# One pair of heads moved between the recurrent tiles, and the last x^T block loaded behind two products, in a hybrid decoder block

## Chip, cores and metric

The kernel runs on one core of a Trainium2 chip. The metric is the time of one execution on the device in microseconds. The engines have the profile's names: PE (TensorE matmul), PEld (its weight loads), DVE (VectorE), ACT (ScalarE), POOL (GpSimd), SP (SyncE, which issues most DMAs).

## What is computed

One decoder block on x of 2048 tokens by 1024, in float32. Cut to what matters here:

```
h = rms_norm(x)
z = h @ w_in                       # 1024 x 2560
q, k, v (512 each), xr (512), gr (512) = split(z)
attn = dilated_attention(q, k, v)  # 8 heads of 64, three dilations
xr   = causal_depthwise_conv(xr)   # 4 taps
rec  = rg_lru(xr) * gelu(gr)       # gated linear recurrence over tokens
m = concat(attn, rec) @ w_out
x = x + rms_norm(m)
x = x + rms_norm(squared_relu_mlp(rms_norm(x)))
```

The recurrence is h = a·h + u along the tokens, with a and u made from two gates (block-diagonal matmuls, then tanh). The MLP is 1024 to 4096 to 1024.

## The kernel before

**Products.** Each float32 operand is split into a high and a low part, both of the matmul's fp32r type, and a product is three matmuls: high by high, low by high, high by low (`product`, L206 to L208). Channels of z are cut into 20 tiles of 128, tokens into two halves `hf` of 1024, each of two blocks b of 512. A product z*hf*_*ct*_*b* takes channel tile ct and one block: 8 slices of the 1024 inputs by 3 matmuls, 24 matmuls of 128x512 into one PSUM bank. The tag "P" of these banks has two buffers, so a product can start only when the one two before it has been read. Tiles 0 to 3 are q, 4 to 7 k, 8 to 11 v (one for each pair of heads), 12 to 15 the recurrence's input, 16 to 19 its gate.

**Weights.** `load_w` brings a tile's weights in two raw halves ("wraw", two buffers), casts them on ACT (wH, L56) and subtracts (wL, L57). The engine of the subtraction is `self.lo`, POOL at first. Behind BETWEEN (below) it is set to VectorE. The low parts of q and k (zl) go by the same setting. After each step of products `load_ahead` loads the next step's first weights.

**Input.** `load_x(tb)` loads eight raw tiles of x^T for 512 tokens (xr, L157), six into the low part's own later slots and two into "wraw", and makes hH (ACT, L180) and hL (VectorE, L181). `spread_norm(tb)` turns the tokens' norm factors into a row for all partitions (four dg, L194, four matmuls, one copy). Blocks 2 and 3 are the second half.

**Steps.** `qkv(hf, pr)`, letter q, makes six products for a pair of heads, multiplies each by the norm row on VectorE (zn, L233 and L236), and stores q, k and v to DRAM. `recurrent(hf, (c,))`, letter r, makes for each block a product of tile 12 + c (VectorE reads it into xr, L312), a convolution (POOL L315, three VectorE steps L318), the two gate matmuls (pr, L321, and pi, L323), ACT functions, the scan (L339), a product of tile 16 + c (VectorE reads it into gr, L343), gelu (POOL L346 to L348, ACT L349, VectorE L350 and L351) and a store. `attend(pr)`, letter a, is the first half's attention for a pair: scores S and SB, masking on VectorE (L422), exp on ACT (L428), transposes pT (L401), output sums oA and oB (L589, L648), normalisers pst (L680).

**What sets the order.** Three strings give the program order:

```
ORDER = "q00 r02 q01 a0 r03 q02 a1 q03 x2 x3 a2 q10 a3"
BETWEEN = "r10 r11 r12 r13"
LATER = "q11 q12 q13"
```

The two digits behind a letter are the half and the pair or tile; x is a load of x^T with its norm row. The scheduler written into the kernel (`Plan` and `Machine`) then orders the instructions of all five engines by its own table of costs and by when each result is needed. A step moved in a string moves several hundred instructions on each engine. q10 has its own order of products: q and k of block 2 before those of block 3.

After BETWEEN the recurrence's pool is closed, and in its room `load_wo(0)` loads W_out: eight loads of 512 KB (woL, L800), each cast in two halves to woH and subtracted. Then the steps of LATER run, five steps of `early_factors` (sums of W_ff tiles, e*j*_*m*) behind each, and what is left of these at the end. The first products that use W_out follow (m, L865 to L867). m0_0_1 means: half 0, token tile 0, columns 1.

Of the kernel before, what the change touches and what calls it, by code (L numbers as in the profile page):

```python
# [39 lines left out]
def f32(ap):  # L40
    return ap.bitcast(F32)
# [12 lines left out]
def split(nc, hi, lo, src, lo_eng=None):  # L54

    return (nc.scalar.copy(out=hi, in_=src),  # L56
            (lo_eng or nc.vector).tensor_tensor(out=lo, in0=src, in1=f32(hi), op=ALU.subtract))  # L57
# [31 lines left out]
class Project:  # L89
# [118 lines left out]
            pe.matmul(z, lo[:, k, :], hh, start=False, stop=(k == KT - 1))  # L208
        return z

    def qkv(self, hf, pr):

        nc, p, scr = self.nc, self.p, self.scr
        v, pe = nc.vector, nc.tensor
        last = hf == 0 and pr == NP - 1
        steps = [(k, b) for k in range(3) for b in range(NBH)]
        if last:

            steps = [(0, 0), (0, 1), (1, 0), (2, 0), (1, 1), (2, 1)]
        elif hf and pr == FIRST:  # L220

            steps = [(0, 0), (1, 0), (0, 1), (1, 1), (2, 0), (2, 1)]
        ws = {}
        for kind, b in steps:
                ct = 4 * kind + pr
                if kind not in ws:
                    ws[kind] = self.load_w(hf, ct)
                w = ws[kind]
                cs = slice(b * TB, (b + 1) * TB)
                z = self.product(hf, ct, w, b)  # L230
                zn = self.pa.tile([P, TB], F32, tag="t512", bufs=3, name=f"zn{hf}_{ct}_{b}")
                if kind == 0:
                    v.scalar_tensor_tensor(out=zn, in0=z, scalar=-(HD ** -0.5), in1=self.bc[b], op0=ALU.mult,  # L233
                                           op1=ALU.mult)
                else:
                    v.tensor_tensor(out=zn, in0=z, in1=self.bc[b], op=ALU.mult)  # L236
                if kind < 2:
                    zh = self.pa.tile([P, TB], F32R, tag="zh", bufs=1, name=f"zh{hf}_{ct}_{b}")
                    zl = self.pa.tile([P, TB], F32R, tag="zl", bufs=1, name=f"zl{hf}_{ct}_{b}")
                    self.cst["pool"] = split(nc, zh, zl, zn, lo_eng=self.lo)[1]  # L240
                    dst = scr["q" if kind == 0 else "k"][hf][pr]
                    for u in range(2):
                        nc.sync.dma_start(out=f32(dst[u, 0, :, cs]), in_=f32(zh[u * HD:(u + 1) * HD, :]))
                        nc.sync.dma_start(out=f32(dst[u, 1, :, cs]), in_=f32(zl[u * HD:(u + 1) * HD, :]))
                else:
                    pt = self.bank("X", f"vt{hf}_{ct}_{b}")
# [597 lines left out]
class OutProj:  # L844
# [1092 lines left out]
def trunk(tc, x, xT, g1, g2, g3, g4, w_in, conv_w, conv_b, w_r, b_r, w_i, b_i, lam, w_out, w1, w2,  # L1937
# [4 lines left out]
    def sb(name, side):  # L1942
        return tc.tile_pool(name=name, bufs=1, side=side, reuse_waits="tile")
# [5 lines left out]
    with (  # L1949
# [46 lines left out]
        def load_wo(hf, between=lambda: None):  # L1996
            return load_w_out(tc, wst.enter_context(sb(f"wo{hf}", "right")), scr["wout"], hf, order, cst, between)

        with contextlib.ExitStack() as st:
            p1a = st.enter_context(sb("p1a", "left"))  # L2000
            p1 = st.enter_context(sb("p1", "left"))
            lst = contextlib.ExitStack()
            pl = lst.enter_context(sb("lru", "left"))
            pj = Project(tc, p1, p1a, pl, bank, cst, scr, x, xT, g1, w_in)
            pj.recurrent_consts(conv_w, conv_b, w_r, b_r, w_i, b_i, lam)
            with sb("x0", "right") as px:
                w = {12: pj.load_start(12, px)}
                z = pj.product(0, 12, w[12], 0, "B")
                w[16] = pj.load_w(0, 16, nc.vector, px)
                w[13] = pj.load_w(0, 13, nc.vector, px)  # L2010
                pj.load_norm(0, px)
                pj.spread_norm(0)
                pj.recurrent_block(0, 0, 0, w[12], w[16], px, z)
                w[17] = pj.load_w(0, 17, nc.gpsimd, px)
                pj.load_x(1, px)
                pj.recurrent_block(0, 1, 0, w[13], w[17], px)
                pj.load_norm(1, px)
                pj.spread_norm(1)
                for i in range(2):
                    pj.recurrent_block(0, i, 1, w[12 + i], w[16 + i], px)  # L2020
                pj.load_norm(2, px)
                pj.load_norm(3, px)
            products = [(t[0], *map(int, t[1:])) for t in f"{ORDER} {BETWEEN} {LATER}".split() if t[0] in "qr"]

            copies = [(scr["wout"][k], w_out[k]) for k in order]
            for j in range(NJ):
                copies += [(scr["w2"][j][:, 0], w2[2 * j][:, 0:TB]),
                           (scr["w2"][j][:, 1:3], w2[2 * j + 1].rearrange("p (a d) -> p a d", a=2))]

            def run(steps):  # L2030
                for kind, *arg in [(t[0], *map(int, t[1:])) for t in steps.split()]:
                    if kind == "q":
                        pj.qkv(*arg)
                    elif kind == "r":
                        pj.recurrent(arg[0], (arg[1],))
                    elif kind == "a":
                        attend(*arg)
                    else:
                        pj.load_x(*arg)
                        pj.spread_norm(*arg)  # L2040
                    n = 8 if kind == "r" and arg[0] else 1 if len(copies) > 2 * NJ else 0
                    with tc.issue_after(cst["pool"].ins):
                        for dst, src in copies[:n]:
                            nc.gpsimd.dma_start(out=dst, in_=src)
                    del copies[:n]
                    if kind in "qr":
                        products.pop(0)
                        if products:
                            nxt, hf, i = products[0]
                            pj.load_ahead(hf, i if nxt == "q" else 12 + i)  # L2050

            place = {"S": ("B", "B"), "pT": ("T", "T"), "o": ("O", "T")}
            with sb("at0", "right") as pa:
                attend = attention(tc, pa, lambda k, n: bank(place[k][0], n), cst, scr, 0, mask_a, mask_b, pa)
                run(ORDER)
            pg = per.enter_context(sb("g2", "right"))
            sh = Shared(pg, bank)
            run(BETWEEN)
            lst.close()
            wo = load_wo(0)  # L2060
            pj.lo = nc.vector
            early = [early_factors(nc, sh, scr, w1, j) for j in range(2)]
            for step in LATER.split():
                run(step)
                for _ in range(5):
                    if early and next(early[0], True):
                        early.pop(0)
            for rest in early:
                for _ in rest:
                    pass  # L2070
            ready = [mix_columns(nc, sh, scr, 0, order, t) for t in range(2)]
# [85 lines left out]

FIRST = 0
SH = 2
ORDER = "q00 r02 q01 a0 r03 q02 a1 q03 x2 x3 a2 q10 a3"  # L2160
BETWEEN = "r10 r11 r12 r13"
LATER = "q11 q12 q13"


def _by_residue(t):
# [53 lines left out]
```

## Time and profile before

| | |
|---|---|
| median of 3 runs | 2226.05 us (2224.66 to 2227.85) |
| profiled execution | 2225.13 us, span 2223.4 us, mean granted clock 0.99 |
| PE busy | 97% of the span, 10264 matmuls |
| DVE, ACT, POOL busy | 69%, 56%, 20% |
| DMA | 473.51 MB, 213 GB/s mean |
| tail of attention 2; end of the last product of z | 341 to 359 us; 637 us |

The profiled execution is 0.9 us shorter than the median. The steps lie in its span as follows: a1 to about 290 us, x2, x3 and a2 to 359, q10 to 388, a3 to 424, r10 to r13 from 412 to 529, q11 to q13 from 529 to 637, the m products after that. Read the table of windows by PE's busy time against a window's length (the rest is idle) and by PEclk (a share below 1 makes the same matmuls take longer).

### The profile page before, as it was taken

The numbers are of one execution on the slowest core, as the hardware profiler recorded it, in microseconds if no ns is written. First come the engines' busy times: TensorE is split into PE (matmuls) and PEld (weight loads), VectorE is DVE, ScalarE is ACT, GpSimd is POOL, SyncE is SP. The second block draws the span as 40 slices with busy tenths as digits, with TensorE's granted clock in tenths as the row PEclk, the third lists the DMA queues.
The fourth block names the chain that finished last, engine by engine and source line by source line (L and its number), as shares of the span: only waits on it lengthen the run. The fifth ranks groups of instructions, "written<-read, shape, count | busy, mean of one in ns | idle before, by whom it ended". The sixth has DMA issues, their size and how long they took to land.

```text
span 2223.4 us, 30885 instructions
## 1 busy us (share of the span) xinstructions
PE 2155.1 (97%) x10264; PEld 1770.1 (80%) x10264; DVE 1529.9 (69%) x2910; ACT 1235.2 (56%) x2487; POOL 454.5 (20%) x536
## 2 busy tenths in 40 slices
PE   8999998988999999999999999999999999999998
PEld 6787877766888788888788888877878888888887
DVE  6858765897647867676567777777766565755556
ACT  6646655645434555555566767754455555654442
POOL 4652434386212100000001111113200000000003
PEclk9999998999999999999999999999999999999999
DMA  7574675247954677779777787786553434876665
GB/s 252 159 220 149 199 236 182 70 163 265 333 167 150 241 269 270 288 269 333 261 220 242 206 246 213 218 256 198 191 175 139 161 132 163 305 219 191 194 194 180
DMA packets 224116, 473.51 MB, mean 213 GB/s; under 512 B 23428, under 2 KB 78756, under 8 KB 217684
## 3 DMA queue, kind: packets, MB, share of 16 engines
q1 hardware_dynamic: 195140, 337.52, 47.7%
q0 software_dynamic: 28816, 134.01, 16.9%
q8 instruction: 81, 1.33, 0.2%
q14 instruction: 79, 0.65, 0.1%
HBM read 337.09 MB, written 151.13 MB: 220 GB/s over the span
## 4 chain that ended last, share of the span: by engine, by line
PE 81%; DVE 9%; ACT 4%; DMA 3%; issue 2%; POOL 1%; SPq 0%; DVEq 0%; ACTq 0%; POOLq 0%
PE o L1230 8%; PE o L1232 8%; PE o L1231 8%; PE za L1081 5%; PE za L1082 5%; PE za L1080 5%; PE z L206 4%; PE z L207 4%; PE z L208 4%; PE m L867 3%; PE m L866 3%; PE m L865 3%; PE zc L1080 2%; PE zc L1082 2%; PE zc L1081 2%
## 5 line engine op out<-in xcount | busy, mean ns | idle before, releaser
L206 PE MATMUL z<-hH,wH 128*128 128x512 f32 x640 | 258.6, 404 | 12.2 <-ACT wH L56 5.3
L208 PE MATMUL z<-hH,wL 128*128 128x512 f32 x640 | 258.6, 404 | 2.5 <-POOL wL L57 2.5
L207 PE MATMUL z<-hL,wH 128*128 128x512 f32 x640 | 256.4, 401 | 0.5 <-DVE hL L181 0.5
L206 PEld LDWEIGHTS z<-hH,wH 128*128 128x128 f32 x640 | 121.8, 190 | 45.0 <-DVE xr L312 6.0
L208 PEld LDWEIGHTS z<-hH,wL 128*128 128x128 f32 x640 | 122.0, 191 | 30.6 <-issue 4.3
L207 PEld LDWEIGHTS z<-hL,wH 128*128 128x128 f32 x640 | 121.6, 190 | 29.7 <-issue 3.1
L1085 ACT ACTIVATE sq<-sq 128x512 f32<-128x512 f32 x93 | 58.8, 632 | 76.1 <-DVE sq L1089 76.1
L428 ACT ACTIVATE smB<-smB,stB 128x128 f32<-128x128 f32 (+3 forms) x128 | 71.5, 560 | 43.2 <-DVE stB L422 43.0
L1145 POOL DMA_DIRECT2D sa<-sq x31 | 16.5, 532 | 375.2 <-ACT sq L1086 368.1
L428 ACT ACTIVATE sm<-sm,stA 128x256 f32<-128x256 f32 (+1 forms) x128 | 63.5, 498 | 49.9 <-DVE stA L422 48.8
L57 POOL TENSOR_TENSOR wL<-wraw,wH 128x512 fp32r<-128x512 f32 x58 | 81.9, 1430 | 36.7 <-ACT wH L56 36.3
L56 ACT CAST wH<-wraw 128x512 fp32r<-128x512 f32 (+1 forms) x81 | 47.1, 611 | 71.5 <-PE z L207 49.9
L1086 ACT ACTIVATE sq<-sq 128x512 f32<-128x512 f32 x124 | 76.9, 630 | 2.6
L57 DVE TENSOR_TENSOR tlB<-pT_B,thB 128x384 fp32r<-128x384 f32 x96 | 57.3, 598 | 28.4 <-ACT thB L56 26.2
L422 DVE CUSTOM_DVE_ANT_0 smB<-SB,mask_b 128x128 f32<-128x128 f32 (+3 forms) x128 | 59.6, 485 | 22.5 <-PE pT_B L401 14.1
L1264 POOL TENSOR_TENSOR y<-y,g4b 128x512 f32<-128x512 f32 x8 | 12.5, 1576 | 257.1 <-ACT junk_y L86 257.1
L422 DVE CUSTOM_DVE_ANT_0 sm<-S,mask_a 128x256 f32<-128x256 f32 (+1 forms) x128 | 48.2, 408 | 24.3 <-PE S L565 22.3
L56 ACT CAST thB<-pT_B 128x384 fp32r<-128x384 f32 x96 | 49.0, 511 | 23.5 <-PE pT_B L401 18.1
L401 PE MATMUL pT_B<-ident,smB 128*128 128x128 f32 x320 | 55.7, 280 | 3.9 <-DVE tlB L57 1.9
L236 DVE TENSOR_TENSOR zn<-z,bc 128x512 f32<-128x512 f32 x32 | 22.0, 686 | 52.8 <-PE z L208 47.9
L867 PE MATMUL m<-woH,m_4L 128*128 128x512 f32 x128 | 51.1, 401 | 3.4 <-DVE m_4L L57 3.4
L1081 PE MATMUL za<-hLT,f_6H 128*128 128x512 f32 x128 | 50.6, 396 | 1.3 <-DVE hLT L57 1.3
(607 smaller groups left out, 7077.2 us busy)
## 6 DMA issues: line engine op xcount, KB each, us to landing
sa<-as POOLq DMA_DIRECT2D x31, 1024.0 KB, 7.2
w1r<-in_dram SPq DMA_DIRECT2D x56, 512.0 KB, 3.7
sa<-sq POOLq DMA_DIRECT2D x31, 768.0 KB, 4.0
wraw<-in_dram SPq DMA_DIRECT2D x79, 256.0 KB, 3.2
place<-in_dram SPq DMA_DIRECT2D x14, 1024.0 KB, 6.7
sb<-place POOLq DMA_DIRECT2D x14, 1024.0 KB, 4.2
kh<-sk SPq DMA_DIRECT2D x24, 512.0 KB, 5.2
kl<-sk SPq DMA_DIRECT2D x24, 512.0 KB, 6.3
```

The source lines that it names most:

```text
L57: (lo_eng or nc.vector).tensor_tensor(out=lo, in0=src, in1=f32(hi), op=ALU.subtract))
L206: pe.matmul(z, hi[:, k, :], hh, start=(k == 0), stop=False)
L207: pe.matmul(z, hi[:, k, :], hl, start=False, stop=False)
L208: pe.matmul(z, lo[:, k, :], hh, start=False, stop=(k == KT - 1))
L428: s.activation(out=sm[:, c0:c0 + w], in_=sm[:, c0:c0 + w], func=AF.Exp, scale=-1.0, bias=st[:, 0, u, cols[j]:cols[j] + 1], accum_out=st[:, ...
L867: pe.matmul(o, ml, wh[:, ds], start=False, stop=(k == order[-1]))
L1080: pe.matmul(o, hi[:, k], bh[:, k], start=start and k == 0, stop=False, skip_group_check=True)
L1081: pe.matmul(o, hi[:, k], bl[:, k], start=False, stop=False, skip_group_check=True)
L1082: pe.matmul(o, lo[:, k], bh[:, k], start=False, stop=k == KH - 1, skip_group_check=True)
L1230: pe.matmul(o, ah[:, ts], bh, start=fresh and j == 0, stop=False, skip_group_check=True)
L1231: pe.matmul(o, ah[:, ts], bl, start=False, stop=False, skip_group_check=True)
L1232: pe.matmul(o, al[:, ts], bh, start=False, stop=j == NJ - 1, skip_group_check=True)
```

## The change

Three things are edited. x3 leaves ORDER, and block 3 is loaded instead inside q10, behind its first two products (z1_0_0 and z1_4_0, which read block 2 only). q11 goes from LATER to BETWEEN, between r11 and r12; W_out's loads and the switch of the low parts' engine, both behind BETWEEN, now come after q11, and two steps q are left in LATER.

```
--- before.py
+++ after.py
@@ -208,7 +208,7 @@
             pe.matmul(z, lo[:, k, :], hh, start=False, stop=(k == KT - 1))
         return z
 
-    def qkv(self, hf, pr):
+    def qkv(self, hf, pr, amid=None):
 
         nc, p, scr = self.nc, self.p, self.scr
         v, pe = nc.vector, nc.tensor
@@ -221,8 +221,10 @@
 
             steps = [(0, 0), (1, 0), (0, 1), (1, 1), (2, 0), (2, 1)]
         ws = {}
-        for kind, b in steps:
+        for n, (kind, b) in enumerate(steps):
                 ct = 4 * kind + pr
+                if amid and n == 2:
+                    amid()
                 if kind not in ws:
                     ws[kind] = self.load_w(hf, ct)
                 w = ws[kind]
@@ -2027,17 +2029,20 @@
                 copies += [(scr["w2"][j][:, 0], w2[2 * j][:, 0:TB]),
                            (scr["w2"][j][:, 1:3], w2[2 * j + 1].rearrange("p (a d) -> p a d", a=2))]
 
+            def load(tb):
+                pj.load_x(tb)
+                pj.spread_norm(tb)
+
             def run(steps):
                 for kind, *arg in [(t[0], *map(int, t[1:])) for t in steps.split()]:
                     if kind == "q":
-                        pj.qkv(*arg)
+                        pj.qkv(*arg, (lambda: load(3)) if arg == [1, FIRST] else None)
                     elif kind == "r":
                         pj.recurrent(arg[0], (arg[1],))
                     elif kind == "a":
                         attend(*arg)
                     else:
-                        pj.load_x(*arg)
-                        pj.spread_norm(*arg)
+                        load(*arg)
                     n = 8 if kind == "r" and arg[0] else 1 if len(copies) > 2 * NJ else 0
                     with tc.issue_after(cst["pool"].ins):
                         for dst, src in copies[:n]:
@@ -2157,9 +2162,9 @@
 
 FIRST = 0
 SH = 2
-ORDER = "q00 r02 q01 a0 r03 q02 a1 q03 x2 x3 a2 q10 a3"
-BETWEEN = "r10 r11 r12 r13"
-LATER = "q11 q12 q13"
+ORDER = "q00 r02 q01 a0 r03 q02 a1 q03 x2 a2 q10 a3"
+BETWEEN = "r10 r11 q11 r12 r13"
+LATER = "q12 q13"
 
 
 def _by_residue(t):
```

All lines of the kernel behind L225 stand two or more lines lower in the changed kernel (L401 is L403, L315 is L317, L800 is L802). The rows below are the instructions as issued, `line operation output<-inputs shape`; the last number of a name only counts tiles.

PE at the end of attention 2, before: S0_6 and pT0_0_6 are already pair 3's attention, z1_4_0 the second product of q10, z1_0_1 its third (it reads block 3).

```order
L565 MATMUL S0_6_4_4137<-kh0_6_4080,qa0_6_4083 128x256
L565 MATMUL S0_6_4_4137<-kl0_6_4081,qa0_6_4083 128x256
L401 MATMUL pT0_0_6_0_0_4102<-ident_60,sm0_6_0_4091 128x128
L206 MATMUL z1_4_0_3869<-hH2_0_3231,wH1_4_3859 128x512
L207 MATMUL z1_4_0_3869<-hL2_0_3232,wH1_4_3859 128x512
L206 MATMUL z1_0_1_3904<-hH3_0_3294,wH1_0_3219 128x512
L207 MATMUL z1_0_1_3904<-hL3_0_3295,wH1_0_3219 128x512
L208 MATMUL z1_0_1_3904<-hH3_0_3294,wL1_0_3220 128x512
L206 MATMUL z1_0_1_3904<-hH3_1_3300,wH1_0_3219 128x512
L208 MATMUL z1_4_0_3869<-hH2_0_3231,wL1_4_3860 128x512
```

PE at the tail of attention 2 after the change: pT0_B0_5 is the transposed probability of pair 2, oA0_5 its output sum.

```order
L591 MATMUL oA0_5_1_3603<-thA0_3577,va0_2_3296 128x128
L591 MATMUL oA0_5_1_3603<-tlA0_3578,va0_2_3296 128x128
L206 MATMUL z1_4_0_3806<-hH2_0_3231,wH1_4_3796 128x512
L207 MATMUL z1_4_0_3806<-hL2_0_3232,wH1_4_3796 128x512
L206 MATMUL z1_0_1_3904<-hH3_0_3843,wH1_0_3219 128x512
L207 MATMUL z1_0_1_3904<-hL3_0_3844,wH1_0_3219 128x512
L403 MATMUL pT0_B0_5_2_0_3677<-ident_60,smB0_5_2_0_3666 128x128 x2
L208 MATMUL z1_4_0_3806<-hH2_0_3231,wL1_4_3797 128x512
L403 MATMUL pT0_B0_5_3_0_3700<-ident_60,smB0_5_3_0_3689 128x128
L206 MATMUL z1_4_0_3806<-hH2_1_3237,wH1_4_3796 128x512
L207 MATMUL z1_4_0_3806<-hL2_1_3238,wH1_4_3796 128x512
```

z1_4_0 has moved from behind pair 3's first scores to among the last transposes and output sums of pair 2; the rest of its 24 matmuls is spread over the rows that follow, before pst0_2.

POOL in r11 before: na0_3 and nb0_3 are outputs of pair 3's attention, wL1_14 and wL1_18 the low weights of r12, ge1_1_0 the gelu of r11's first block.

```order
L726 TENSOR_TENSOR na0_3_4068<-na0_3_4068,co0_3_0_4517 128x512
L729 TENSOR_TENSOR nb0_3_4069<-nb0_3_4069,co0_3_0_4517 128x512
L353 DMA smix1_104<-ge1_0_1_4717 128x512
L732 TENSOR_TENSOR na0_3_4068<-na0_3_4068,nb0_3_4069 128x512
L315 TENSOR_SCALAR xc1_1_1_4870<-xr1_1_1_4866,cw_222,vec_cb_224 128x512
L57 TENSOR_TENSOR wL1_14_4938<-wraw1_14_0_4939,wH1_14_4937 128x512
L346 TENSOR_TENSOR ge1_1_0_4833<-gr1_1_0_4831 128x512
L347 TENSOR_SCALAR ge1_1_0_4833<-ge1_1_0_4833 128x512
L348 TENSOR_TENSOR ge1_1_0_4833<-ge1_1_0_4833,gr1_1_0_4831 128x512
L57 TENSOR_TENSOR wL1_14_4938<-wraw1_14_1_4943,wH1_14_4937 128x512
L57 TENSOR_TENSOR wL1_18_4948<-wraw1_18_0_4949,wH1_18_4947 128x512
```

POOL in r11 after the change: wL1_1 and wL1_5 are the low weights of q11's q and k.

```order
L728 TENSOR_TENSOR na0_3_4068<-na0_3_4068,co0_3_0_4517 128x512
L57 TENSOR_TENSOR wL1_1_4938<-wraw1_1_0_4939,wH1_1_4937 128x512
L317 TENSOR_SCALAR xc1_1_1_4870<-xr1_1_1_4866,cw_222,vec_cb_224 128x512
L348 TENSOR_TENSOR ge1_1_0_4833<-gr1_1_0_4831 128x512
L57 TENSOR_TENSOR wL1_1_4938<-wraw1_1_1_4943,wH1_1_4937 128x512
L349 TENSOR_SCALAR ge1_1_0_4833<-ge1_1_0_4833 128x512
L350 TENSOR_TENSOR ge1_1_0_4833<-ge1_1_0_4833,gr1_1_0_4831 128x512
L57 TENSOR_TENSOR wL1_5_5018<-wraw1_5_0_5019,wH1_5_5017 128x512
L731 TENSOR_TENSOR nb0_3_4069<-nb0_3_4069,co0_3_0_4517 128x512
L57 TENSOR_TENSOR wL1_5_5018<-wraw1_5_1_5023,wH1_5_5017 128x512
L734 TENSOR_TENSOR na0_3_4068<-na0_3_4068,nb0_3_4069 128x512
```

Four halves of q11's weights stand where r12's stood, and behind them, further on, come its other low parts. They were on VectorE before.

SP at the loads of W_out before: sk1_1 and sv1_1 are the stores of q11's k and v, wraw1_10 the raw weights of q12's v.

```order
L243 DMA sk1_1_84<-zh1_5_0_5522 64x512 x2
L244 DMA sk1_1_84<-zl1_5_0_5523 64x512 x2
L252 DMA sv1_1_92<-vs1_9_0_5607 128x4x256
L800 DMA woL0_6_5370<-swo6_207 128x1024
L800 DMA woL0_7_5368<-swo7_208 128x1024
L157 DMA wraw1_10_0_5851<-in_6_dram 128x512
L157 DMA wraw1_10_1_5855<-in_6_dram 128x512
L800 DMA woL0_0_5366<-swo0_201 128x1024
L800 DMA woL0_1_5364<-swo1_202 128x1024
L243 DMA sk1_1_84<-zh1_5_1_5557 64x512 x2
```

SP at the end of these loads after the change: wraw1_11 are the raw weights of q13's v, sq1_3 the store of q13's q, m0_0_4L a tile of the mixer's output.

```order
L802 DMA woL0_6_5612<-swo6_207 128x1024
L157 DMA wraw1_11_1_6097<-in_6_dram 128x512
L802 DMA woL0_7_5610<-swo7_208 128x1024
L802 DMA woL0_0_5608<-swo0_201 128x1024
L839 DMA m0_0_4L_6245<-smix0_103 128x4x128
L245 DMA sq1_3_78<-zh1_3_0_5968 64x512 x2
L802 DMA woL0_1_5606<-swo1_202 128x1024
L246 DMA sq1_3_78<-zl1_3_0_5969 64x512 x2
L802 DMA woL0_2_5604<-swo2_203 128x1024
L802 DMA woL0_3_5602<-swo3_204 128x1024
```

The loads stood among q11's and q12's stores and weights, and stand now among q12's and q13's. The last two, woL0_2 and woL0_3, are issued behind the store of zl1_3_0, the low part of q13's q.

More of the change, by code (lines that the diff above doesn't have):

```diff
@@ L209, in product, with qkv @@
         return z
-    def qkv(self, hf, pr):
+    def qkv(self, hf, pr, amid=None):
         nc, p, scr = self.nc, self.p, self.scr
@@ L223, in qkv @@
         ws = {}
-        for kind, b in steps:
+        for n, (kind, b) in enumerate(steps):
                 ct = 4 * kind + pr
+                if amid and n == 2:
+                    amid()
                 if kind not in ws:
@@ L2028, in trunk, with load @@
                            (scr["w2"][j][:, 1:3], w2[2 * j + 1].rearrange("p (a d) -> p a d", a=2))]
+            def load(tb):
+                pj.load_x(tb)
+                pj.spread_norm(tb)
             def run(steps):
@@ L2032, in run @@
                     if kind == "q":
-                        pj.qkv(*arg)
+                        pj.qkv(*arg, (lambda: load(3)) if arg == [1, FIRST] else None)
                     elif kind == "r":
@@ L2038, in run @@
                     else:
-                        pj.load_x(*arg)
-                        pj.spread_norm(*arg)
+                        load(*arg)
                     n = 8 if kind == "r" and arg[0] else 1 if len(copies) > 2 * NJ else 0
@@ L2159 @@
 SH = 2
-ORDER = "q00 r02 q01 a0 r03 q02 a1 q03 x2 x3 a2 q10 a3"
-BETWEEN = "r10 r11 r12 r13"
-LATER = "q11 q12 q13"
+ORDER = "q00 r02 q01 a0 r03 q02 a1 q03 x2 a2 q10 a3"
+BETWEEN = "r10 r11 q11 r12 r13"
+LATER = "q12 q13"
 def _by_residue(t):
```

## The prediction

> **What bounds the kernel now.** I read the profile's page first, for the engine that sets the time.
>
> ```profile
> span 2223.4 us, 30885 instructions
> ...
> PE 2155.1 (97%) x10264; PEld 1770.1 (80%) x10264; DVE 1529.9 (69%) x2910; ACT 1235.2 (56%) x2487; POOL 454.5 (20%) x536
> ...
> PE 81%; DVE 9%; ACT 4%; DMA 3%; issue 2%; POOL 1%; SPq 0%; DVEq 0%; ACTq 0%; POOLq 0%
> ```
>
> TensorE is idle for 68.3 of 2223.4 us and is 81% of the chain that ended last. A move that leaves TensorE's work alone can win only idle time and time at a low clock. So the second view is the table of windows, cut at the steps that the change touches. Columns: window, its length, busy time (instructions) of the five engines, granted clock, DMA share, GB/s.
>
> ```profile
> core 0: us, PE busy (x) PEld busy (x) DVE busy (x) ACT busy (x) POOL busy (x), PEclk, DMA share, GB/s
> 248.00:285.00 37.00, 36.30 (x259) 31.03 (x259) 29.42 (x99) 31.02 (x95) 5.10 (x5) 1.00 0.66 209
> 308.80:314.00 5.20, 0.06 (x2) 0.06 (x1) 5.20 (x7) 0.49 (x3) 4.92 (x4) 0.99 0.86 231
> 314.00:341.00 27.00, 26.45 (x181) 23.56 (x181) 22.62 (x85) 25.44 (x78) 1.07 (x2) 0.94 0.57 195
> 341.00:359.00 18.00, 12.62 (x70) 10.41 (x69) 14.70 (x33) 10.82 (x28) 1.28 (x2) 0.62 0.77 234
> 359.00:388.00 29.00, 29.00 (x138) 24.18 (x137) 8.65 (x21) 9.35 (x24) 20.60 (x18) 1.00 0.56 173
> 426.00:466.00 40.00, 37.08 (x155) 28.43 (x154) 36.15 (x41) 17.38 (x23) 30.93 (x29) 1.00 0.46 152
> 466.00:530.00 64.00, 56.24 (x206) 40.90 (x205) 52.13 (x64) 32.06 (x42) 50.97 (x56) 0.92 0.57 189
> 530.00:560.00 30.00, 27.85 (x118) 21.73 (x117) 24.18 (x36) 16.43 (x25) 16.01 (x24) 1.00 0.88 306
> 560.00:600.00 40.00, 40.00 (x181) 33.06 (x180) 29.30 (x46) 19.82 (x37) 10.08 (x16) 1.00 1.01 358
> ```
>
> There are two places to win. **The tail of pair 2's attention (341 to 359)** has 70 attention matmuls and not one product beside them: 18 − 12.62 = 5.4 us idle, and 12.62 × 0.38 = 4.8 us lost to the clock of 0.62, 10.2 us together. **The recurrent tiles (426 to 560)** lose 2.9 + 7.8 + 2.2 = 12.9 us idle and 56.24 × 0.08 = 4.5 us of clock, 17.4 us together. The stall at 308.8 to 314 lies before the first row that the change moves, and I leave it in. From 560 on TensorE is full, so what is hidden there can only be uncovered.
>
> Next, whom TensorE waits for, in the waits from 300 to 400 us and then from 440 to 560 us (us in total, times, longest).
>
> ```profile
> PE S L565 <- DVE stA L422: 5.3, 2, 5.1
> PE oB L648 <- DVE nb L417: 1.7, 1, 1.7
> PE pst L680 <- DVE nb L417: 1.4, 1, 1.4
> PE pT_B L401 <- DVE tlA L57: 1.3, 2, 1.1
> ```
>
> ```profile
> PE z L206 <- DVE xr L312: 4.1, 3, 2.1
> PE pr L321 <- DVE xc L318: 2.9, 1, 2.9
> PE z L208 <- POOL wL L57: 2.5, 1, 2.5
> PE z L206 <- DVE zn L233: 1.6, 1, 1.6
> PE pi L323 <- ACT r L326: 1.1, 2, 0.5
> PE z L206 <- DVE gr L343: 0.6, 1, 0.6
> ```
>
> In the attention tail the waits are steps of one chain (softmax on DVE and ACT, transposes, output sums), and nothing independent stands between them. In the recurrent stretch a product waits until VectorE has emptied an earlier product's bank (xr L312, gr L343, zn L233): VectorE is behind. In 426 to 530 it is busy 36.15 + 52.13 = 88.3 of 104 us, and the idle grows from window to window, as a backlog does.
>
> **Part 1: x3 behind the first two products.** The order of instructions in the section on the change shows the program's answer: z1_4_0 moves into the tail of attention 2. A product is 24 matmuls, and the dense window 560 to 600 gives 40.00/181 = 0.221 us for each, so 5.3 us: as much as the tail's 5.4 us of idle. No matmul is added; what was done after 359 is done before. If all gaps are filled and the clock stays up, the gain is 10.2. If z1_4_0 only fills gaps, the clock stays low and one half of its weight's low part is waited for on POOL, the gain is 5.4 − 1.4 = 4.0, the price of that half being this mean:
>
> ```profile
> L57 POOL TENSOR_TENSOR wL<-wraw,wH 128x512 fp32r<-128x512 f32 x58 | 81.9, 1430 | 36.7 <-ACT wH L56 36.3
> ```
>
> The nearest row is 248 to 285, an earlier attention with products between its steps: 36.30 of 37.00 busy at clock 1.00. It is close to the upper end. I take 9, less than 10.2, since here one product stands in the tail and there more than one. The eight x^T loads, their ACT and VectorE steps and the norm row come along with the move. The loads of k = 6 and 7 go from before raw tile 1_4 to behind it on SP; they are covered by z1_4_0 itself, 5.3 us. If that cover fails, the nearest price is the stall at 308.8 to 314, 5.1 us, which would eat half the term. It is in the lower end.
>
> **Part 2: q11 between r11 and r12.** Six products of q11 (about 32 us of TensorE) need from VectorE only six short reads and two subtractions of v; a recurrent block needs over a dozen VectorE steps. So VectorE works off its backlog while TensorE runs products. Which gaps go? Four starts after a gap in the timeline (start, us, what, [idle before <- releaser]):
>
> ```profile
> 455.39 1.10 PE L321 MATMUL pr<-xc,bd_r 128*128 128x512 f32 x2 [2.92 <-DVE xc L318]
> 470.00 0.50 PE L208 MATMUL z<-hH,wL 128*128 128x512 f32 x1 [2.50 <-POOL wL L57]
> 505.18 0.79 PE L206 MATMUL z<-hH,wH 128*128 128x512 f32 x1 [1.68 <-DVE xr L312]
> 521.83 0.56 PE L206 MATMUL z<-hH,wH 128*128 128x512 f32 x1 [2.10 <-DVE xr L312]
> ```
>
> The first belongs to r11, the second to r12, the last two to r13. After the change r11 keeps its 2.9. r12 starts with VectorE level, as r10 did, which shows no wait in the list above: 0.3. r13 then stands where r11 stands now or worse; I keep its own gaps, 3.8, and one of the three drops of the clock, 4.5/3 = 1.5, so 5.3. q11 in its new place follows one gap rather than four: 0.8. q12 now follows r13 and inherits part of q11's 2.2: 1.3. Left over: 2.9 + 0.8 + 0.3 + 5.3 + 1.3 = 10.6, a gain of 17.4 − 10.6 = 6.8. I take 6, since q11's low parts go from VectorE to POOL (its engine is switched only after BETWEEN): six halves of weights and four of q and k. Their prices, the halves on POOL in 426 to 530 and one on VectorE:
>
> ```profile
> L57 POOL TENSOR_TENSOR wL<-wraw,wH 128x512 fp32r<-128x512 f32 x14 | 21.6, 1562 | 4.8 <-ACT wH L56 4.8
> ...
> 529.63 0.69 DVE L57 TENSOR_TENSOR wL<-wraw,wH 128x512 fp32r<-128x512 f32 x1 [1.57 <-ACT wH L56]
> ```
>
> That is 10 × 1.56 = 15.6 us more on POOL and 10 × 0.69 = 6.9 us less on VectorE. POOL has room: 30.93 of 40 and 50.97 of 64 us. Bounds of this term: 0 (nothing gained) to 17.4 − 2.9 = 14.5 (only r11's gap is left). Five early-factor steps of W_ff lose their place behind q11 and come after q13, where TensorE is full from products; I cost them at nothing. Without that cover each is a step of 0.7 us on VectorE.
>
> One of the prices of a gap is the clock. The window at 0.62 has gaps of 1.7 us at most and the window at 0.92 of 2.5, while the 2.92 at 455.39 lies in a window at 1.00. The Trainium skill, TensorE: Matmul & The Clock Gate, section HAM oscillation, puts it as no PE-idle gaps above about 3.4 us; the windows here do not agree, since shorter gaps went with a low clock. By that rule r13's clock term would be 0 and the forecast 1.5 us lower.
>
> **Part 3: W_out comes closer to its use.** The first m product stays twelve z products behind z1_19_1: those of q11 and q12 before, those of q12 and q13 after. The rows, z1_19_1 being the one that starts at 521.83 above:
>
> ```profile
> 557.87 1.08 DVE L351 SCALAR_TENSOR_TENSOR ge<-ge,xc 128x512 f32<-128x512 f32 x1
> ...
> 559.42 1.57 SPq L800 DMA_DIRECT2D woL<-swo  x2
> ...
> L57 DVE TENSOR_TENSOR woL<-woL,woH x16: 681/685/694, 571.2 to 594.7; 128x512 fp32r<-128x512 f32 x16
> L800 SPq DMA_DIRECT2D woL<-swo x8: 319/724/1837, 559.4 to 584.0; - x8
> ...
> DMA to landing us min/median/max: 7.1/7.6/9.4
> ...
> 599.79 0.39 PE L865 MATMUL m<-woH,m_0H 128*128 128x512 f32 x1
> ```
>
> The room is freed with the last L351 of r13, 36 us after z1_19_1 starts; the loads leave SP 38 to 62 us after it, the last subtraction starts at 73 us and the first m product at 78. Without q11's gaps (2.2) those thirteen products take 76 us, 5.8 each. After the change SP holds the last two of the eight loads behind the write of q's low part of pair 3 (zl1_3_0), which stands on VectorE behind the read of z1_7_0, the ninth product after z1_19_1: 10 × 5.8, and some 2 for the read, the cast and the subtraction (0.69 each) make 60; issue at 62, landing 9.4 at the slowest, four subtractions of 0.69: 74. The m products start at 76, and by the order these two tiles are used 24 matmuls later, at 81. The slack is 7 us. I charge 1 for a start that isn't clean; bounds 0 and 8 (all eight loads as late as the slowest landing).
>
> **The sum.** 9 + 6 − 1 = 14. The profiled execution took 2225.13 (span 2223.4, 1.7 outside it), so 2211.1; the median of the runs, 2226.05, is 0.9 above that execution, so the forecast is **2212**.
>
> **The rivals.**
>
> *VectorE and POOL share a limit.* Then moving q11's low parts to POOL slows VectorE by as much as q11 relieves it, and part 2 is 0: 2226.05 − 9 + 1 = 2218. For it, a pair on VectorE during 303.9 to 312.7, with POOL at work, beside the mean of the same step from 341 to 359, with POOL nearly idle:
>
> ```profile
> 303.90 8.77 DVE L181 SCALAR_TENSOR_TENSOR hL<-xr,g_sb,hH 128x512 fp32r<-128x512 f32 x2 [1.36 <-ACT hH L180]
> 305.93 2.54 POOL L57 TENSOR_TENSOR wL<-wraw,wH 128x512 fp32r<-128x512 f32 x2
> ...
> L181 DVE SCALAR_TENSOR_TENSOR hL<-xr,g_sb,hH 128x512 fp32r<-128x512 f32 x5 | 3.7, 748 | 0.1
> ```
>
> 8.77 us against 2 × 0.75. Against it: in 466 to 530 VectorE was busy 52 of 64 us with POOL at 51 of 64, so both get through. Chance 0.18. The Trainium skill, GPSIMD Engine Reference, section 1. Specifications, has GpSimd's SBUF interfaces shared with VectorE, in contention with instructions of two SBUF inputs; the two L181 above agree.
>
> *The tail stays a chain, and the backlog comes back.* Part 1 gives 4, part 2 only 2: 2226.05 − 4 − 2 + 1 = 2221. For it, the waits in the tail are on results one after another; against it, 248 to 285. Chance 0.10.
>
> *Both stretches become dense.* 10.2 + 14.5 − 0: 2201.4. Against it, r11's neighbours r12 and r13 still follow each other. Chance 0.12.
>
> *W_out arrives late (slower).* The place is the first m product, the price one us of TensorE for each us by which the last tiles lag beyond the slack of 7. With parts 1 and 2 won (15 us) the time is 2226.05 − 15 = 2211, and it passes 2230.5 when they lag by 7 + 19.5 = 26.5 us. For it, VectorE finished r13 36 us behind the start of z1_19_1, as long as six products, and the write of zl1_3_0 stands on SP ahead of the last two loads; against it, q12's products need little of VectorE. With a lag of 28 it gives 2232. Chance 0.05.
>
> That the change does not do what it says is excluded by the order of instructions, which shows both moves.
>
> **How the numbers follow.** About 0.2% (4.45 us) can be told from no change in this kernel. The forecast has 0.55, with its own range 2206 to 2217. Faster by over 0.2% means below 2221.6: all of the forecast, the dense case, 0.15 of the first rival and 0.04 of the second, 0.86. Within 0.2%: 0.09. Slower: 0.05. The range from the dense case to the second rival, 2202 to 2221.5, leaves out half of the dense case, part of the second rival and the slow one.
>
> **What would show it.** Right: in the windows of the changed kernel the attention tail has z1_4_0's 24 matmuls in it and a clock above 0.9; r12 shows no wait on xr L312 (L314 there); the m products start within 2 us of the last z product. Wrong: the tail still shows idle of 5 us or a clock of 0.6 (part 1); z products of r12 wait on VectorE or on POOL's wL as before (part 2); m waits on woL (part 3).

## The result, and the profile after

The changed kernel took 2201.15 us (median of 4, 2196.84 to 2207.02) against 2225.45 for the kernel before, a ratio of 0.9891 with a 95% interval of 0.9866 to 0.9916: 24 us faster. The forecast was 2212 with a range of 2202 to 2221.5, so the time lies just under the range. Run again with the experiments it took 2202.75 (6 executions, 2191.84 to 2207.17). The profiled execution took 2202.12, its span 2200.3.

The page of the changed kernel first.

```profile
span 2200.3 us, 30893 instructions
...
PE 2146.3 (98%) x10264; PEld 1765.9 (80%) x10264; DVE 1535.4 (70%) x2900; ACT 1235.7 (56%) x2487; POOL 467.0 (21%) x546
```

TensorE runs the same 10264 matmuls and is idle for 54.0 us where it was 68.3. POOL has ten instructions more, VectorE ten fewer: q11's low parts. Next the same windows as in the prediction.

```profile
core 0: us, PE busy (x) PEld busy (x) DVE busy (x) ACT busy (x) POOL busy (x), PEclk, DMA share, GB/s
308.80:314.00 5.20, 1.76 (x13) 1.35 (x13) 4.44 (x10) 1.76 (x7) 4.14 (x4) 1.00 0.93 273
341.00:359.00 18.00, 17.81 (x109) 14.36 (x110) 16.06 (x33) 10.68 (x26) 5.97 (x4) 1.00 0.94 281
426.00:466.00 40.00, 38.57 (x157) 28.82 (x156) 36.57 (x42) 19.64 (x27) 30.27 (x28) 1.00 0.52 167
466.00:530.00 64.00, 60.42 (x254) 47.53 (x253) 44.85 (x46) 26.66 (x39) 41.55 (x48) 0.97 0.63 214
530.00:560.00 30.00, 28.91 (x119) 21.72 (x118) 29.25 (x42) 17.48 (x25) 20.86 (x30) 1.00 0.70 250
600.00:640.00 40.00, 40.00 (x181) 33.07 (x181) 27.31 (x48) 16.88 (x36) 11.59 (x8) 1.00 0.80 265
```

The attention's tail, 341 to 359, is full at a clock of 1.00; it was busy 12.62 at 0.62. 51 product matmuls stand there, where none stood before. From 426 to 560 the idle is 6.1 us and the low clock costs 60.42 × 0.03 = 1.8; before, 12.9 and 4.5. TensorE's waits from 440 to 560 us:

```profile
PE pr L323 <- DVE xc L320: 2.5, 2, 1.4
PE vt L250 <- DVE zn L238: 2.5, 1, 2.5
PE z L206 <- DVE zn L235: 0.9, 1, 0.9
```

No z product waits for xr or gr any more. The wait of 2.9 at pr1_1_0, the gate matmul of r11's first block, has gone as well, which was not forecast; the 1.4 is at that of its second block, pr1_1_1, which now stands among q11's products.

Where the 23.1 us of the two profiled executions lie is told by the lengths between the same marks in all of them (end of S0_4_4, z1_8_1, z1_16_1, z1_17_1 and m0_3_0, and of the span; from the named rows of each timeline). The kernels below the second row are the experiments.

| kernel | to S0_4_4 | tail of a2, q10 | a3, r10 | r11 | rest of the products, W_out | rest |
|---|---|---|---|---|---|---|
| before | 316.2 | 70.9 | 48.3 | 28.9 | 209.3 | 1549.8 |
| changed | 314.0 | 61.5 | 48.2 | 25.6 | 201.9 | 1549.1 |
| a2_same | 310.2 | 60.7 | 48.2 | 25.6 | 198.4 | 1547.9 |
| e1_x3_only | 315.8 | 60.4 | 48.2 | 25.6 | 213.6 | 1552.6 |
| e2_q11_only | 316.7 | 71.6 | 48.4 | 30.0 | 200.1 | 1549.7 |
| e3_q11_vector | 311.6 | 62.4 | 48.2 | 25.6 | 210.4 | 1549.8 |
| e4_x3_q11_pool | 316.6 | 60.4 | 48.1 | 25.6 | 220.9 | 1550.0 |
| e5_q11_late | 317.5 | 60.3 | 48.1 | 25.6 | 208.9 | 1548.1 |
| e6_q11_early | 312.2 | 61.1 | 48.2 | 227.5 with the next | | 1547.0 |
| e7_two | 316.2 | 60.9 | 48.2 | 25.6 | 196.5 | 1550.9 |
| e8_break | 312.9 | 59.6 | 48.5 | 27.2 | 208.1 | 1544.9 |
| e9_pair3_vector | 311.8 | 72.3 | 48.4 | 26.0 | 209.3 | 1547.6 |
| e10_two_break | 314.8 | 60.5 | 48.5 | 27.2 | 199.5 | 1552.8 |
| e11_two_pair3 | 316.2 | 60.7 | 48.2 | 25.6 | 195.9 | 1546.5 |

The gain is 2.2 + 9.4 + 0.1 + 3.3 + 7.4 + 0.7 = 23.1. The last column, which no edit touches, spans 8 us over the kernels, so one execution's total is not evidence. The middle columns are, beyond the 3.5 us by which the two executions of the changed kernel (second and third row) differ in the fifth.

### The profile page after: what moved, and what is told of

Read it like the earlier page. It is cut to its first block, busy times and chain, and to the rows that moved or that the text cites. A ratio compares the mean times of both kernels' runs of the same rounds, so it can differ in the third digit from the quotient of the medians.

```text
span 2200.3 us, 30893 instructions
## 1 busy us (share of the span) xinstructions
PE 2146.3 (98%) x10264; PEld 1765.9 (80%) x10264; DVE 1535.4 (70%) x2900; ACT 1235.7 (56%) x2487; POOL 467.0 (21%) x546
## 4 chain that ended last, share of the span: by engine, by line
PE 81%; DVE 7%; ACT 3%; DMA 3%; POOL 2%; issue 2%; SPq 0%; DVEq 0%; POOLq 0%; ACTq 0%
PE o L1232 9%; PE o L1233 8%; PE o L1234 8%; PE za L1083 5%; PE za L1084 5%; PE za L1082 5%; PE z L207 4%; PE z L206 4%; PE z L208 4%; PE m L869 3%; PE m L868 3%; PE m L867 3%; PE zc L1082 2%; PE zc L1083 2%; PE zc L1084 2%
## 5 line engine op out<-in xcount | busy, mean ns | idle before, releaser
L57 POOL TENSOR_TENSOR wL<-wraw,wH 128x512 fp32r<-128x512 f32 x64 | 88.0, 1386 | 68.2 <-ACT wH L56 67.7
L430 ACT ACTIVATE sm<-sm,stA 128x256 f32<-128x256 f32 (+1 forms) x128 | 63.5, 498 | 48.4 <-DVE stA L424 47.4
L403 PE MATMUL pT_B<-ident,smB 128*128 128x128 f32 x320 | 54.4, 278 | 3.7 <-DVE tlA L57 1.7
L320 DVE SCALAR_TENSOR_TENSOR xc<-xr,cw,xc 128x512 f32<-128x512 f32 x48 | 51.4, 1077 | 5.9 <-POOL xc L317 5.8
```

Of the source, the lines that this page charges most:

```text
L430: s.activation(out=sm[:, c0:c0 + w], in_=sm[:, c0:c0 + w], func=AF.Exp, scale=-1.0, bias=st[:, 0, u, cols[j]:cols[j] + 1], accum_out=st[:, ...
```

## The experiments

Times are medians, with the ratio to the kernel before on the same chip and its 95% interval.

**The parts apart, and the engine of q11's subtractions.** Four kernels were made:

```diff
 e1_x3_only, against the changed kernel
-BETWEEN = "r10 r11 q11 r12 r13"
-LATER = "q12 q13"
+BETWEEN = "r10 r11 r12 r13"
+LATER = "q11 q12 q13"
 e2_q11_only, against the kernel before
-BETWEEN = "r10 r11 r12 r13"
-LATER = "q11 q12 q13"
+BETWEEN = "r10 r11 q11 r12 r13"
+LATER = "q12 q13"
 e3_q11_vector, against the changed kernel (e4_x3_q11_pool: the same on e1, with gpsimd)
+                        lo = pj.lo
+                        if arg == [1, 1]:
+                            pj.lo = nc.vector
                         pj.qkv(*arg, (lambda: load(3)) if arg == [1, FIRST] else None)
+                        pj.lo = lo
```

Expected of e1:

> The x3 move alone; q11 stays behind r13. Theory (the two parts work in different places and add): the gain up to the end of r11 stays, as in the changed kernel (z1_17_1 ends 15.0 us earlier, 449.3 against 464.3), and r12, r13 and q11 lose what they lost before: 2225 - 15 = 2210, and W_out has its old place. Rival (the gain in the recurrent tiles comes from the new order that any move brings, the gate matmuls standing later among the products): most of the other 10 us comes too, 2202 or less. Rival (the tail of attention 2 was only worth its 5.4 us of idle): 2219.

Measured: 2217.92, ratio 0.9972 (0.9954 to 0.9990). Up to the end of r11 the theory held: the tail gave 10.5 and r11 3.3, without q11 between the tiles. But the stretch behind it took 4.3 us more than before (213.6 against 209.3). Its waits from 440 to 560:

```profile
PE pi L325 <- ACT r L328: 4.3, 3, 2.7
PE z L206 <- DVE xr L314: 3.0, 2, 1.5
PE pr L323 <- DVE xc L320: 2.7, 1, 2.7
PE z L206 <- DVE gr L345: 1.9, 1, 1.9
PE z L206 <- DVE state L342: 0.9, 2, 0.7
```

The new order put the gate matmuls elsewhere among r12's and r13's products, and they wait there. The rival "a new order helps by itself" falls: here it cost. The total missed the theory's 2210 by 8 us, of which this stretch is 4.3, and lies near the other rival's 2219, whose reason does not hold: the tail gave 10.5 and not 5.4.

Expected of e2:

> q11 between r11 and r12 alone; x3 stays before attention 2. Theory (the parts add): the tail of attention 2 keeps its 10 us of loss, r11 keeps its wait of 2.9 us, r12 and r13 lose 10.4 us less and the W_out stretch 2.9 us more: 2225 - 7.5 = 2217.5. Rival (it helps only after the order that the x3 move brings): within 3 us of 2225.

Measured: 2217.86, ratio 0.9965 (0.9949 to 0.9980), as the theory had it; r11 took 30.0, its wait in place (2.8 at pr1_1_0), and the stretch behind it gained 9.2. So each part alone is worth some 6 us, and both together 22 to 24: the x3 move alone gives back part of its gain between r12 and q11, and q11's place takes that loss away.

Expected of e3:

> The changed kernel with q11's ten subtractions on VectorE instead of POOL. Theory (the place of q11 gives the gain; VectorE works off its lag during q11 whoever subtracts): 2201 within 3 us. Rival (the relief is the 10 x 0.69 = 6.9 us taken off VectorE): the gain of r12 and r13 shrinks by about 7, 2208. Second rival (POOL and VectorE hinder each other): faster than 2201 by 2 to 6 us, the VectorE steps of the recurrence shorter than in the changed kernel (the three convolution steps 1.30 us on the mean there).

Measured: 2209.05, ratio 0.9931 (0.9904 to 0.9958). That is the first rival's number, 6 to 8 us above the medians of the changed kernel. The ratios' intervals just overlap, but the stretch behind r11 took 210.4 where the changed kernel's two executions took 201.9 and 198.4. The products keep the changed kernel's order: VectorE reads q11's six products (zn) before r12's first (xr). The last two of these reads and the first of r12, with the step ahead of which VectorE waited:

```profile
479.54 0.69 DVE L238 TENSOR_TENSOR zn<-z,bc 128x512 f32<-128x512 f32 x1 [0.23 <-PE z L208]
487.27 1.08 DVE L352 SCALAR_TENSOR_TENSOR ge<-ge,gr 128x512 f32<-128x512 f32 x1 [7.04 <-ACT ge L351]
...
490.45 0.68 DVE L238 TENSOR_TENSOR zn<-z,bc 128x512 f32<-128x512 f32 x1
...
498.05 1.07 DVE L314 TENSOR_TENSOR xr<-z,bc 128x512 f32<-128x512 f32 x1 [3.81 <-PE z L208]
```

So where the subtractions run does matter here. But the rival's reason, a VectorE with more to do, is not what the rows show: from 426 to 560 VectorE is busy 109.2 of 134 us, in the changed kernel 110.7, and ahead of TensorE's longest wait (4.0 us, at vt1_9_1, for the zn at 490.45) VectorE itself sat idle for 7.04 us. From r11's second block on the scheduler also orders much else differently, and which part of that costs the time was not isolated.

Expected of e4:

> The x3 move alone, q11 behind r13 as before, but q11's subtractions on POOL. Theory (place): same as the x3 move alone within 2 us. Rival (relief of VectorE by POOL): 4 to 7 us faster than the x3 move alone.

Measured: 2221.56, ratio 0.9983 (0.9966 to 1.0000): 4 us slower than e1, against the rival, and more than the theory's 2 us. Its longest wait is 4.4 us at z1_1_1, for a zn on VectorE. Taking ten subtractions off VectorE was no relief here.

**The place of q11.** a2_same is the changed kernel itself. The edits of the other three are lines of the strings:

```diff
 e5_q11_late
+BETWEEN = "r10 r11 r12 q11 r13"
 e6_q11_early
+BETWEEN = "r10 q11 r11 r12 r13"
 e7_two
+BETWEEN = "r10 r11 q11 r12 q12 r13"
+LATER = "q13"
```

> The changed kernel once more, as the measure for the others on the same chip: 2201 within 3 us. If VectorE's step hL2_5 is held by POOL's row of subtractions for a varying time (5.97 us in its profile, 7.16 before, 1.78 with q11 on VectorE), single executions spread by up to 5 us.

Measured: 2202.75, ratio 0.9889 (0.9857 to 0.9921). Its profiled execution, 2192.76, has no stall at S0_4_4 and no wait of 2.5 at vt1_9_1, with the same instructions in the same order.

> The changed kernel with q11 between r12 and r13 in the strings. The order of products is now that of the run with q11's subtractions on VectorE (there the kernel's scheduler also put r12 ahead of q11), so the two differ in the engine of the subtractions. Theory (place: what counts is that the lag is worked off between tiles): 2209 within 3 us, as that run. Rival (the subtractions on POOL are worth the 8 us): 2201 within 3.

Measured: 2208.85, ratio 0.9919 (0.9889 to 0.9948). That this is e3's time, 2209.05, says nothing on the engine, since the expectation has e3's order wrong: there q11 stands ahead of r12, here behind it, as the last read of r12's input and q11's first read show:

```profile
481.09 1.05 DVE L314 TENSOR_TENSOR xr<-z,bc 128x512 f32<-128x512 f32 x1
...
497.00 0.68 DVE L235 SCALAR_TENSOR_TENSOR zn<-z,bc 128x512 f32<-128x512 f32 x1
```

What e5 tests is the place, against a2_same, which has the subtractions on POOL as well: 6.1 us slower, and 208.9 us in the stretch behind r11 against 201.9 and 198.4. The ratios' intervals of e5 and a2_same overlap, so the totals alone would not settle it.

> The changed kernel with q11 between r10 and r11. Theory (place; lag of VectorE behind the gate product is 18 to 21 us after r10 and 30 to 40 after r11): q11 comes when there is little lag to work off, r11 to r13 follow each other and the last two lose about 5 us: 2206. Rival (any place between the tiles does): 2201 within 3.

Measured: 2204.98, ratio 0.9903 (0.9876 to 0.9930). Forecast 2206, but its interval holds the rival's 2201 as well. The stretch of r11 and the rest is 227.5, the changed kernel's 227.5 and a2_same's 224.0: inconclusive.

> The changed kernel with q12 moved too, between r12 and r13: only six products, 33 us, are left between r13 and the first product that uses W_out. Theory (W_out's room is free only after r13's last VectorE step, some 36 us after its last product, so the m products wait): r13 wins 2 to 3 us, W_out costs 8 to 18: 2207 to 2217. Rival (W_out's loads follow faster when nothing is queued ahead of them on SP): 2198 to 2202.

Measured: 2199.16, ratio 0.9879 (0.9853 to 0.9904): the rival. The theory of a late W_out fell. The tiles of W_out in this kernel (count, duration min/median/max, first and last start):

```profile
L56 ACT CAST woH<-woL x16: 612/619/624, 598.0 to 611.5; 128x512 fp32r<-128x512 f32 x16
L57 DVE TENSOR_TENSOR woL<-woL,woH x16: 671/681/684, 602.6 to 614.0; 128x512 fp32r<-128x512 f32 x16
L802 SPq DMA_DIRECT2D woL<-swo x8: 319/465/1291, 593.6 to 602.3; - x8
```

The eight loads leave SP within 8.7 us, where they were spread over 24.6 before, and the first m product starts at 607.76 with no wait in the list from 600 to 660. With q11 and q12 between the tiles, TensorE is busy all 30.00 us from 530 to 560 and 63.71 of 64 before that, and 39.12 of 40 from 560 to 600, where most of r13 now lies:

```profile
466.00:530.00 64.00, 63.71 (x276) 50.67 (x275) 44.72 (x52) 31.11 (x46) 45.41 (x52) 1.00 0.72 240
530.00:560.00 30.00, 30.00 (x137) 24.44 (x136) 27.82 (x29) 9.27 (x17) 24.72 (x32) 1.00 0.95 322
```

**What held VectorE.** The stall at S0_4_4 differs from execution to execution, and r11's wait went with the x3 move. Both looked like a VectorE that has too much to do. The rows say otherwise: a single step is held, that is, recorded as under way for several times what it usually takes. VectorE and POOL of the kernel before, in r11 (start, us):

```profile
448.72 1.77 DVE L318 SCALAR_TENSOR_TENSOR xc<-xr,cw,xc 128x512 f32<-128x512 f32 x1
450.42 4.18 DVE L339 TENSOR_TENSOR_SCAN xc<-r,state,i 128x512 f32<-128x512 f32 x1
454.52 0.72 DVE L318 SCALAR_TENSOR_TENSOR xc<-xr,cw,xc 128x512 f32<-128x512 f32 x1
```

```profile
449.89 1.09 POOL L2044 DMA_DIRECT2D sw<-in_dram  x2
450.99 1.30 POOL L726 TENSOR_TENSOR na<-na,co 128x512 f32<-128x512 f32 x1
452.24 1.27 POOL L729 TENSOR_TENSOR nb<-nb,co 128x512 f32<-128x512 f32 x1
```

The scan takes 4.18 us and ends when the two steps L726 and L729 of pair 3's attention have ended (453.51) and 1.1 us more have passed, about what a scan lasts. The last convolution step behind it is what pr1_1_0 waited for. The test takes the two steps, and the four like them, away from POOL:

```diff
 e9_pair3_vector, against the kernel before
-        e = v if hf else g
+        e = v if hf or pr == 3 else g
```

> The kernel before, with the six steps that combine pair 3's outputs on VectorE instead of POOL; around r11's wait TensorE's and VectorE's orders stay as they are. Theory (r11's wait of 2.9 us came from the scan L339, held for 4.18 us by two of these steps on POOL, not from VectorE's own load): the scan takes under 2.2 us and the wait of the gate matmul pr1_1_0 falls below 1 us; 2 to 3 us less up to the end of r11, about 2222 in all. Rival (VectorE has too much to do): with 6 x 0.69 = 4.1 us more on it the wait stays or grows, and the time is 2225 or more.

Measured: 2219.93, ratio 0.9977 (0.9961 to 0.9993). TensorE's and VectorE's orders there are those of before up to the moved steps. VectorE of this kernel:

```profile
445.82 1.77 DVE L318 SCALAR_TENSOR_TENSOR xc<-xr,cw,xc 128x512 f32<-128x512 f32 x1
447.52 1.27 DVE L339 TENSOR_TENSOR_SCAN xc<-r,state,i 128x512 f32<-128x512 f32 x1
448.71 0.72 DVE L318 SCALAR_TENSOR_TENSOR xc<-xr,cw,xc 128x512 f32<-128x512 f32 x1
```

The scan takes 1.27 us, the wait at pr1_1_0 is gone and r11 takes 26.0 instead of 28.9, with the same VectorE steps ahead of it: of the six moved ones the first three start at 451.80, behind the scan. The theory held. The total fell by 5.5 us; where it won more than these 2.9 is not located, and its profiled execution had no stall at S0_4_4. In the kernels with the x3 move the same two steps stand behind the scan: in e1 the first starts at 443.83, the scan at 439.21, for 1.27 us. That is where r11's 3.3 us come from.

The stall at S0_4_4 looks like the same thing in another place. Two of VectorE's steps L181 took 8.77 us in the prediction's row; in the changed kernel's profile, with POOL's row beside it:

```profile
304.56 6.84 DVE L181 SCALAR_TENSOR_TENSOR hL<-xr,g_sb,hH 128x512 fp32r<-128x512 f32 x2 [1.58 <-ACT hH L180]
```

```profile
309.58 1.26 POOL L728 TENSOR_TENSOR na<-na,co 128x512 f32<-128x512 f32 x1
311.82 1.28 POOL L731 TENSOR_TENSOR nb<-nb,co 128x512 f32<-128x512 f32 x1 [0.98 <-DMA co<-sco]
```

POOL waited 0.98 us for a DMA from 310.84 on, and VectorE's pair ended at 311.40. In the kernel before no such gap came, and it ended at 312.67:

```profile
309.64 1.25 POOL L726 TENSOR_TENSOR na<-na,co 128x512 f32<-128x512 f32 x1
310.86 1.25 POOL L729 TENSOR_TENSOR nb<-nb,co 128x512 f32<-128x512 f32 x1
312.19 1.60 POOL L732 TENSOR_TENSOR na<-na,nb 128x512 f32<-128x512 f32 x1
```

In e3's execution POOL was later than VectorE by chance (its two wL start at 308.31), and the pair took 2.45 us with no stall:

```profile
305.51 2.45 DVE L181 SCALAR_TENSOR_TENSOR hL<-xr,g_sb,hH 128x512 fp32r<-128x512 f32 x2 [1.36 <-ACT hH L180]
```

Three more kernels used this:

```diff
 e8_break, against the changed kernel (e10_two_break: the same on e7)
+                            lo, pj.lo = pj.lo, nc.vector if (nxt, hf, i) == ("q", 1, 0) else pj.lo
                             pj.load_ahead(hf, i if nxt == "q" else 12 + i)
+                            pj.lo = lo
 e11_two_pair3, against e7
-        e = v if hf else g
+        e = v if hf or pr == 3 else g
```

> The changed kernel with the low part of q10's first weights (two subtractions, wL1_0) on VectorE instead of POOL, so that POOL's unbroken row behind 305 us is split. Theory (a VectorE step with two operands that starts beside such a row is held until the row breaks; hL2_5 took 5.97 us in the changed kernel, 7.16 before, 1.78 and no stall in one run): hL2_5 takes under 2 us, TensorE's stall of 3.4 to 5.1 us at S0_4_4 is below 1 us, and the median is 2 to 4 us under the changed kernel's 2202.5, about 2199, with less spread. Rival (the stall comes from x^T or from VectorE's own work): two more steps of 0.69 us on VectorE, 2202 to 2204, and the stall stays.

Measured: 2210.33, ratio 0.9935 (0.9914 to 0.9956): slower than the changed kernel, a miss. The stall did shrink, to 1.15 us, with hL2_5, the second step of the pair, down to 1.84 us and hL2_4, the first, held for 2.27. But the rows of POOL and VectorE differ far behind the two moved subtractions too, and another step was held in r12, with TensorE waiting 4.4 us for it at z1_19_1:

```profile
535.18 3.68 DVE L353 SCALAR_TENSOR_TENSOR ge<-ge,xc 128x512 f32<-128x512 f32 x1
```

```profile
535.44 2.49 POOL L57 TENSOR_TENSOR wL<-wraw,wH 128x512 fp32r<-128x512 f32 x2
```

The profiled execution, 2202.96, is the fastest of the six, so its rows cannot show the whole loss.

> q11 and q12 both between the recurrent tiles and the low part of q10's first weights on VectorE. Theory: the kernel with both steps moved, 2199.2, less the 2 to 4 us of the stall: 2196. Rival: the two gains overlap, 2199 within 2.

Measured: 2198.75, ratio 0.9889 (0.9866 to 0.9912): the rival, no gain over e7; in its profiled execution hL2_4 was held for 4.04 us and the stall was 3.4, with the same edit that left 1.15 in e8.

> q11 and q12 both between the recurrent tiles, and the six steps that combine pair 3's outputs on VectorE instead of POOL. Theory (holds by POOL cost only where TensorE waits for the held step): with products between the tiles only 1.4 us of wait at pr1_1_1 is left there to win, so 2198 against 2199.2 for the kernel without the second edit. Rival (holds cost VectorE in general, and so the time): the 5 us that the same edit gave the kernel before come here too, 2194.

Measured: 2193.21, ratio 0.9869 (0.9852 to 0.9885), the fastest kernel of the study. The number is the rival's, the place is not: in the stretches that the edit touches it gained 0.6 us (195.9 against 196.5), and 4.4 us lie behind m0_3_0, in code that is the same in both. By the ratios, 0.9869 and 0.9879 on two chips, the two kernels differ by 2 us, and the intervals overlap. Whether the edit is worth anything on top of e7 stays open.

## Why the prediction missed

| term | forecast | measured, profiled pair |
|---|---|---|
| stall at 308.8 to 314 | 0 | 2.2 |
| tail of attention 2 | 9 | 9.4 |
| r11's wait | 0 ("r11 keeps its 2.9") | 3.3 |
| q11 between the tiles, less W_out | 6 − 1 = 5 | 7.4 |
| elsewhere | 0 | 0.8 |
| sum | 14 | 23.1 |

*Part 1* was right in mechanism and size: products filled the tail, the clock rose to 1.00, and over all kernels with the move the stretch was 8.5 to 11.3 us shorter.

*The step that failed* is "VectorE is behind", as the one reason for TensorE's waits on it. From it followed that r11 keeps its wait, since no product is put in before r11, and that a wait ahead of the first moved row cannot change. By the rows neither wait was a backlog. Each was one VectorE step held by a row of POOL steps (4.18 us for a scan that takes 1.27; 7.16 for a step that takes 0.75), and where POOL's rows fall depends on the order, which the x3 move changed, and on the moment at which a DMA lands. e9 shows this for r11's wait: the row was taken away, and the wait went with VectorE's steps ahead of it unchanged. For the stall at 308.8 it is argued and not shown: it rests on executions that had the same instructions there and differed in POOL's timing, and the edit meant to test it left 1.15 us in e8 and 3.4 in e10. Nor is the 2.2 of the table shown to come from the change: the stall lasts 0 to 5.3 us over the profiled executions with the x3 move, so this term is largely luck of the pair. The reading behind the step was weak as well: the idle that "grows from window to window" is 7%, 12% and 7% of the three windows. Whether the other waits of before, in r12 and r13, were holds too was not taken apart.

*Part 2* came out near its worked-out sum but in other places. Of 17.4 us the forecast left 10.6, that is 7.7 behind r11's wait; the changed kernel lost 5.9 of waits and 1.8 of clock there, 7.7. But r13 has no wait above 0.15, where 5.3 was forecast, r12 has 1.1 where 0.3 was, and among q11's products stand two, 1.4 (at pr1_1_1) and 2.5, where 0.8 was; the 2.5 is again a step of VectorE (L353, 4.09 us) beside three POOL subtractions. The 0.3 of r12 was read from r10, by a list that starts at 440, behind most of r10; the waits from 410 on show none of r10's either. Two deductions were not needed. The 0.8 for the subtractions on POOL had the wrong sign: with them on VectorE and the products in the same order (e3) the time was 6 to 8 us longer, for a reason that stays open. And the 1 for W_out was not paid. In the changed kernel's profile W_out's loads leave at 577.0 to 600.9, and the m products start at 610.94 without a wait.

*The rivals.* The limit that VectorE and POOL share was the right mechanism with the wrong sign: it was priced as a loss that the change adds, and it was part of the loss that the change removed. The dense case, 10.2 + 14.5, gave 2201.4, the measured time to 0.3 us, but its bound for part 2 was not reached; the stall and r11's wait made up the number, so it was met by luck. The late W_out is refuted by e7, which leaves only six products ahead of it. That place matters is supported by e5 against the changed kernel (7 to 10.5 us in the stretch); why r12 behind q11 is better than r13 behind q11 was not isolated.

The range's end, 2202.0, lay among the ten executions of the changed kernel, 2191.8 to 2207.2. The spread has a cause that the profile shows in part, the stall that comes or stays away, and the range had not allowed for it.

## What to carry to other kernels

When a VectorE step in the trace lasts several times its usual time, look at POOL in the same microseconds before calling VectorE overloaded; in r11 the wait behind it went when the POOL row was moved, with VectorE's own steps left as they were. Products that need little of VectorE, put between stages in which TensorE waits for single VectorE steps, make such holds harmless without removing them: in e7 VectorE steps of 3.38 and 4.73 us still start at 447.47 and 468.69, and TensorE's waits from 440 to 560 add up to 1.7. And where a scheduler orders the engines, two edits are not the sum of two runs: each alone gave 6 us here, both 22 to 24.

## What the runs showed of the hardware

A VectorE step with POOL steps of two operands in SBUF beside it can be held through several of them: 7.16 us through five (before, where it ended 0.5 us after POOL's first pause, of 0.08 us), 5.97 us through four in the changed kernel, which ended in POOL's pause of 0.98 us, and 4.18 us through two (the scan). The Trainium skill, SBUF — State Buffer, section SBUF: two separate sides, states that VectorE and GpSimd share a port pair by an exclusive lock, and that the later instruction blocks until the earlier one ends. The runs agree that one of them blocks, but by the recorded starts it is not always the later one: the scan starts 0.57 us and hL2_5 of before 0.42 us ahead of the first of the POOL steps that it waits through, while POOL still issues DMAs (449.89 to 450.98 above). That a step stays blocked over a row of instructions that follow each other without a pause, that section of the Trainium skill does not say.
